# A batched product of 96 heads: where the pieces stored apart are multiplied and copied

## The chip, the cores and the metric

The kernel runs on one core of a Trainium2 chip. Its time is device microseconds of one execution. The median of three runs before the change is 300.72 us (300.61 to 300.89).

## The reference

```python
batch, n_heads, seq_t, seq_s, channels = 8, 12, 512, 512, 64
def reference(x, y):            # x: b h t c, y: b h s c, float32
    return np.einsum('bhtc,bhsc->bhts', x, y).astype(np.float32)
```

There are 96 heads. For each, the 512x64 matrix x is multiplied by the transpose of the 512x64 matrix y, which gives 512x512 numbers. 25 MB are read and 100 MB are written.

## The kernel before

The heads are worked off in six loads of 16 heads, for x and for y (`load`, line 157). ScalarE, VectorE and GpSimd turn them to bf16 in one large SBUF tensor, `keep` (`compress`). Each load gives two halves, so there are 12 halves `i` (0 to 11). For each half, `mix` copies x into `xb` in an order fit for the transposes, and `transposes` lets VectorE turn it into `xT` (line 206) and y into `yT` (line 215). `xT` and `yT` exist twice, for even and odd halves.

Each half holds four heads for each of two output rows: the output has 48 tiles `o`, four to a half. A tile is 128 partitions of 4096 numbers, 2 MB. It is made in two halves of four products each (128x128 by 128x512): the first in the PSUM buffer `pm0`, the second in `pm1` (`four`, line 234). Each PSUM buffer is four banks, and the two fill PSUM. ScalarE evicts each half into one of five SBUF slots (`result`, line 337), and SyncE stores the slot (`store`, line 328). A slot is free for another tile when its store has landed.

The order on each engine is written out by hand. `need` finds which semaphores an engine must wait for, and `emit` records who wrote and who reads each buffer. Only TensorE's program is a loop: `all_products` runs six turns of eight tiles each (two halves), and what must run once stands in it as a block under a condition on the turn; `emit(..., held=...)` collects the steps of that block in place of issuing them. Behind the last tile of each half, `prepare` issues the transposes of a later half and the `mix` copies of the one after it.

Tile 41 (`SPLIT`) is stored in parts. All its odd partitions (1 MB) and the first quarter of its even ones (256 KB) leave from the slot. The rest, 64 rows of 12 KB, is made once more in other partitions: `corner` gathers the columns of `xT` that belong to these rows into `picked` (three VectorE copies, line 275), multiplies them by `yT` in 30 products of 96 or 16 columns, four to a group (line 295, eight groups), copies each group into a part of `keep` that is free by then (`kept`, lines 139 and 141), and sends these rows in three transfers: 20 rows by SyncE, 12 and 32 by GpSimd (line 314). The three gathers and the products stand behind tile 41. The groups alternate between `pm0`, copied by VectorE, and `pm1`, copied by ScalarE. TensorE leaves the block when the last copies are done, and only then goes on with tile 42. SyncE issues its 20 rows ahead of the store of tile 42.

Of the kernel before, what the change touches and what calls it, by code (L numbers as in the profile page):

```python
# [9 lines left out]
def kernel(  # L10
# [22 lines left out]
    nc = tc.nc  # L33
    B, H, T, C = x.shape
    _, _, S, _ = y.shape
# [3 lines left out]
    R = T // Q  # L39
# [9 lines left out]
    LEFT = 6  # L49
    N = (K - LEFT) * S  # L50
    GROUP = 4
    FEW = ((0, 4, 5), (5, 8, 4), (16, 24, 4))
    fp32 = mybir.dt.float32
    bf16 = mybir.dt.bfloat16
    u32 = mybir.dt.uint32
# [52 lines left out]
    def emit(name, make, reads=(), writes=(), dma=None, lane=None, known_by=None, held=None):  # L108

        points = [writer[r] for r in (*reads, *writes) if r in writer]  # L110
        points += [v for w in writes for v in readers.get(w, ())]
        if name == "pool" and name in ticks:
            points.append((name, ticks[name]))
        need(name, points, known_by, held)
        p, step = (lane or name, 1) if dma is None else (f"dma{dma}", 16)
        if p not in sems:
            sems[p] = tc.alloc_semaphore(p)
        if held is not None:
            held.append(make)
        elif make is not None:  # L120
            make().then_inc(sems[p], step)
        at = (p, ticks.get(p, 0) + step)
        ticks[p] = at[1]
        snaps[at] = {**known[name], p: at[1]}
        if dma is None:
            for q in lanes.get(name, (name,)):
                snaps[at][q] = ticks.get(q, 0)
        for r in reads:
            readers.setdefault(r, []).append(at)
        for w in writes:  # L130
            writer[w], readers[w] = at, []

    made_slots, loaded, held = [], {}, []
    in_front = ["dve", "pool", "dve", "act"]

    def copy(name, dst, src, reads, writes):
        emit(
            name,
            lambda: nc.scalar.activation(dst, src, COPY)  # L139
            if name == "act"  # L140
            else engines[name].tensor_copy(dst, src),  # L141
            reads,
            writes,
        )
# [95 lines left out]
    def all_products():  # L240

        with nc.tensor.Fori(0, TURNS, 1) as t:
            for j in range(2 * V):
                if j % V == 0:
                    nc.tensor.wait_ge(sems["tr"], t * 2 + j // V + 1)
                for pm in range(2):
                    nc.tensor.wait_ge(sems["ev"], t * (4 * V) + 2 * j + pm + 1)
                    four(j, pm).then_inc(sems["pe"], 1)
                if j == SPLIT % (2 * V):
                    with nc.tensor.If(t == SPLIT // (2 * V)):  # L250
                        for step in held:
                            if callable(step):
                                step().then_inc(sems["pe"], 1)
                            else:
                                nc.tensor.wait_ge(sems[step[0]], step[1])

    def corner():

        half, h = divmod(SPLIT % (2 * V), V)
        xT = xTs[half].bitcast(bf16).rearrange("p (k h q u) -> p k h q u", k=K, h=V, u=2)  # L260
        yT = yTs[half].bitcast(bf16)
        most = max(many for _, _, many in FEW)
        kept = keep[:, :most * LEFT * S].bitcast(fp32)
        runs = kept.rearrange("p (j n) -> p j n", j=most)
        dst = ov[SPLIT // V, h][:, 0, N:]
        picked = keep[:, 3 * NG * R // 2 * D:].bitcast(bf16)[:, :most * LEFT * 96].rearrange(
            "p (j k m) -> p j k m", j=most, k=LEFT
        )
        under = [("yb", 1, b, ch) for b in range(NG - 3, NG - 1) for ch in range(2)]
        first = 0  # L270
        for lo, hi, many in FEW:
            rows = (hi - lo) * many
            emit(
                "dve",
                lambda: nc.vector.tensor_copy(  # L275
                    picked[:, :many, :, 4 * lo:4 * hi:4],
                    xT[:, K - LEFT:, h, first:first + rows, 0].rearrange("p k (e j) -> p j k e", j=many),
                ),
                [("xT", half)],
                [("picked", lo)] + (under if lo == 0 else []),  # L280
            )
            first += rows
        places = [[("xk", i)] for i in range(NG - 1)]
        for i in range(0, NG - 1, 2):
            places.append([("yb", 0, b, ch) for b in (i, i + 1) if b < NG - 1 for ch in range(2)])
        banks = [divmod(b, LEFT) for b in range(most * LEFT)]
        for g in range(0, len(banks), GROUP):
            part = banks[g:g + GROUP]
            pm = g // GROUP % 2
            m = 96 if part[0][0] < most - 1 else 16  # L290

            def make(part=part, pm=pm, m=m):

                for b, (j, k) in enumerate(part):
                    last = nc.tensor.matmul(  # L295
                        pms[pm][:m, b, :], picked[:, j, k, :m], yT[:, h * S:(h + 1) * S],
                        start=True, stop=True,
                    )
                return last

            emit("pe", make, [("picked", lo) for lo, _, _ in FEW] + [("yT", half)], [("pm", pm)], held=held)
            copy(
                "act" if pm else "dve", kept[:m, g * S:(g + len(part)) * S],
                pms[pm].rearrange("p j s -> p (j s)")[:m, :len(part) * S],
                [("pm", pm)], places[g // GROUP],
            )
        need("pe", [v for pm in range(2) for v in readers[("pm", pm)]], held=held)
        first = 0
        for lo, hi, many in FEW:
            rows = (hi - lo) * many  # L310
            name = "pool" if lo else "sp"
            emit(
                name,
                lambda: engines[name].dma_start(  # L314
                    dst[first:first + rows].rearrange("(e j) n -> e j n", j=many),
                    runs[4 * lo:4 * hi - 3:4, :many],
                ),
                reads=[w for place in places for w in place],
                dma="side" if lo else "corner",
            )  # L320
            first += rows
# [24 lines left out]
    def prepare(i):  # L346

        if i < NH:
            transposes(i)
        if i + 1 < NH:  # L350
            for part in range(4):
                mix(i + 1, "dve", part)

    with tc.tile_critical():  # L354
        sems["ev"] = tc.alloc_semaphore("ev")
        ticks["ev"] = 2
        nc.scalar.sem_inc(sems["ev"], 2)
        for g in range(SLOTS):
            load(g)
        emit(  # L360
            "pool",
            lambda: nc.gpsimd.dma_start(  # L362
                spare[0:17:4, :, :D // 2], xv[0, 0:5].rearrange("p (a b c) -> p a b c", a=2, c=D)[:, :, 0, :D // 2]
            ),
            writes=["spare"],
            dma="side",
        )
        for half, name in enumerate(("dve", "pool")):
            emit(
                name,  # L370
                lambda: engines[name].memset(xbs[half], 0.0),  # L371
                writes=[("xb", half, part) for part in range(4)],
            )
        front = []
        for n in range(2 * NG):
            if n == 11:
                result(3, slot())
            compress(n)
            mix(n // 4, "pool", n % 4)
            if n == 4:  # L380
                transposes(0)
            if n < 5:
                load(n + SLOTS)
            elif n in (6, 8):
                load(n // 2 + 7)
            elif n < 10:
                front.append(slot())
            if n > 7 and n < 11:
                result(n - 8, front[n - 8])
            if n == 9:  # L390
                transposes(1)
        prepare(2)
        for o in range(V, V * NH):
            result(o, slot())
            if o == SPLIT:
                corner()
            if o % V == V - 1:
                prepare(o // V + 2)
        all_products()
        need("pool", [("dmaside", ticks["dmaside"])])  # L400
        need("dve", [("dmacorner", ticks["dmacorner"])])
        for i, name in enumerate(("dve", "dve", "dve", "dve", "act")):
            need(name, [(f"dma{i}", ticks[f"dma{i}"])])
# [30 lines left out]
```

## Time and profile before

| | |
|---|---|
| median of three runs | 300.72 us |
| the profiled execution | 300.63 us |
| its span in the trace | 298.8 us |
| mean granted TensorE clock | 0.77 |
| moved by DMA | 125.87 MB, mean 421 GB/s |
| busy: TensorE, VectorE, ScalarE, GpSimd | 48%, 54%, 73%, 19% |
| ScalarE's evictions (line 337) | 96, 173.7 us, mean 1894 ns |
| VectorE's copies of pieces | 4, mean 2285 ns |
| ScalarE's copies of pieces | 4, mean 1657 ns |
| TensorE's products for pieces (line 295) | 30, 9.2 us busy |

A row of the profile names the engine, the line of the kernel, the operation, and what it writes and reads. PE is TensorE's matmul, PEld its weight load, DVE is VectorE, ACT ScalarE, POOL GpSimd, SP SyncE; a "q" behind the name is its sequencer. In brackets stands the idle time of the engine before the row, and what ended it. The slices cut the span in 40 equal parts of 7.47 us; digits are tenths busy, PEclk is the granted clock in tenths. Times are counted from the span's start.

### The profile page before, as it was taken

Reading aid. Unit: us, or ns where it says so; the run is one execution under the profiler, and the core shown is the slowest. Engines: PE = TensorE matmul, PEld = TensorE weight load, DVE = VectorE, ACT = ScalarE, POOL = GpSimd, SP = SyncE. Lnnn points to the kernel's source line nnn. Section 1 sums busy time; section 2 is a strip of 40 time slices with the busy share of each in tenths; the row PEclk is TensorE's granted clock in tenths of the full one; section 3 lists DMA queues with packets and bytes.
Section 4 is the critical chain, followed back from the end, with each engine's and each line's share of the span. In section 5 each row is a group of like instructions: output and inputs, shape, how many; then the busy total and the mean of one; then the engine's idle time right before and its main releaser. Section 6 shows DMA issues by size and latency. Waiting matters only on the chain.

```text
span 298.8 us, 1363 instructions
## 1 busy us (share of the span) xinstructions
PE 144.7 (48%) x408; PEld 39.3 (13%) x414; DVE 161.6 (54%) x80; ACT 217.9 (73%) x113; POOL 57.9 (19%) x26
## 2 busy tenths in 40 slices
PE   0000040547665663867475665676475667475400
PEld 0000010111111110211111111111111112121100
DVE  2167897999929594915809439076292535600000
ACT  1665676999999996786868686767777775589900
POOL 3399999991000000000000000000000000010000
PEclk9999995657789997565956767756857767979965
DMA  7999999999999999999999999999999999999997
GB/s 265 430 428 432 430 430 428 428 432 432 425 432 430 434 428 429 434 430 428 430 432 429 432 436 428 430 436 423 425 432 434 430 421 428 421 388 430 421 421 316
DMA packets 8875, 125.87 MB, mean 421 GB/s; under 512 B 1128, under 2 KB 1128, under 8 KB 1192
## 3 DMA queue, kind: packets, MB, share of 16 engines
q1 hardware_dynamic: 8680, 125.29, 98.6%
q0 software_dynamic: 192, 0.54, 0.5%
q8 instruction: 1, 0.02, 0.0%
q14 instruction: 2, 0.02, 0.0%
HBM read 25.17 MB, written 100.66 MB: 421 GB/s over the span
## 4 chain that ended last, share of the span: by engine, by line
DMA 54%; ACT 27%; issue 5%; PE 4%; DVE 3%; another core or an unknown queue 1%; SPq 0%; ACTq 0%
DMA out_dram<-slot 41%; ACT slot L337 25%; DMA slot<-in_y_dram 7%; DMA slot<-in_x_dram 6%; DVE keep L141 3%; ACT keep L139 2%; PE pm L295 2%; PE pm L234 2%; SPq L157 0%; ACTq L101 0%; SPq L429 0%; SPq L354 0%
## 5 line engine op out<-in xcount | busy, mean ns | idle before, releaser
L337 ACT ACTIVATE slot<-pm 128x2048 f32<-128x2048 f32 x96 | 173.7, 1894 | 38.2 <-DMA out_dram<-slot 35.0
L234 PE MATMUL pm<-yT,xT 128*128 128x512 bf16 x378 | 135.6, 502 | 132.0 <-ACT slot L337 92.4
L206 DVE STREAM_TRANSPOSE xT<-xb 128x2048 uint32<-128x2048 uint32 x12 | 46.8, 3897 | 69.4 <-PE pm L234 67.0
L234 PEld LDWEIGHTS pm<-yT,xT 128*128 128x128 bf16 x384 | 35.9, 114 | 230.7 <-ACT slot L337 152.0
L139 ACT ACTIVATE keep<-slot 128x4096 bf16<-128x4096 f32 (+1 forms) x12 | 36.5, 3044 | 21.5 <-DMA slot<-in_x_dram 16.3
L141 DVE COPY xb<-keep 32x2048 bf16<-32x2048 bf16 x36 | 47.0, 1305 | 1.0
L141 DVE CAST keep<-slot 64x2048 bf16<-64x2048 f32 x12 | 36.1, 3010 | 17.1 <-DMA slot<-in_y_dram 16.9
L314 POOL DMA_DIRECT2D out_dram<-keep x2 | 1.1, 558 | 192.6 <-DVE keep L141 192.6
L141 POOL COPY xb<-keep 32x2048 bf16<-32x2048 bf16 x12 | 36.2, 3017 | 9.2 <-ACT keep L139 8.4
L215 DVE STREAM_TRANSPOSE yT<-keep 128x1024 uint32<-128x1024 uint32 x12 | 23.1, 1928 | 0.0
L141 POOL CAST keep<-slot 64x2048 bf16<-64x2048 f32 x6 | 17.8, 2973 | 1.4 <-DMA slot<-in_y_dram 0.8
L141 DVE COPY keep<-pm 96x2048 f32<-96x2048 f32 (+1 forms) x4 | 9.1, 2285 | 10.5 <-PE pm L295 10.5
L295 PE MATMUL pm<-yT,keep 128*96 128x512 bf16 (+1 forms) x30 | 9.2, 446 | 4.9 <-DVE keep L141 2.8
L139 ACT ACTIVATE keep<-pm 96x2048 f32<-96x2048 f32 (+1 forms) x4 | 6.6, 1657 | 5.4 <-PE pm L295 5.4
L295 PEld LDWEIGHTS pm<-yT,keep 128*96 128x96 bf16 (+1 forms) x30 | 3.4, 130 | 11.0 <-DVE keep L141 4.5
L371 DVE MEMSET xb<- 128x2048 uint32 x1 | 1.8, 1765 | 1.4 <-SPq L354 1.4
L139 ACT ACT_TABLE_LOAD x1 | 1.3, 1283 | 1.0 <-SPq L354 1.0
L371 POOL MEMSET xb<- 128x2048 uint32 x1 | 1.8, 1823 | 0.0
L362 POOL DMA_DIRECT2D spare<-in_x_dram x1 | 0.7, 701 | 1.2 <-SPq L354 1.2
L275 DVE COPY keep<-xT 128x120 bf16<-128x120 bf16 (+2 forms) x3 | 0.7, 355 | 0.0
L418 POOL MEMSET const-float32-0.0<- 128x1 f32 x1 | 0.1, 98 | 0.2 <-issue 0.2
L418 POOL MEMSET const-float32-1.0<- 128x1 f32 x1 | 0.1, 98 | 0.0
(2 smaller groups left out, 0.2 us busy)
## 6 DMA issues: line engine op xcount, KB each, us to landing
out_dram<-slot SPq DMA_DIRECT2D x47, 2048.0 KB, 20.5
slot<-in_x_dram SPq DMA_DIRECT2D x6, 2048.0 KB, 17.7
slot<-in_y_dram SPq DMA_DIRECT2D x6, 2048.0 KB, 20.8
out_dram<-slot SPq DMA_DIRECT2D x1, 1024.0 KB, 16.9
out_dram<-keep POOLq DMA_DIRECT2D x1, 384.0 KB, 6.1
out_dram<-slot SPq DMA_DIRECT2D x1, 256.0 KB, 18.6
out_dram<-keep SPq DMA_DIRECT2D x1, 240.0 KB
out_dram<-keep POOLq DMA_DIRECT2D x1, 144.0 KB, 5.6
```

The lines of the kernel that those rows point to most:

```text
L139: lambda: nc.scalar.activation(dst, src, COPY)
L141: else engines[name].tensor_copy(dst, src),
L206: lambda: nc.vector.transpose(xTs[half].rearrange("p (k r e) -> p k e r", k=K, e=E), xbs[half].rearrange("p (k e c) -> p k e c", k=K, e=E),),
L215: lambda: nc.vector.transpose(yTs[half].rearrange("p (r j) -> p j r", r=D), ybs[half][b].rearrange("p (j c) -> p j c", c=D),),
L234: last = nc.tensor.matmul(pms[pm][:, b, :], xT[:, 4 * pm + b, h, :], yT[:, h * S:(h + 1) * S], start=True, stop=True,)
L275: lambda: nc.vector.tensor_copy(picked[:, :many, :, 4 * lo:4 * hi:4], xT[:, K - LEFT:, h, first:first + rows, 0].rearrange("p k (e j) -> p ...
L295: last = nc.tensor.matmul(pms[pm][:m, b, :], picked[:, j, k, :m], yT[:, h * S:(h + 1) * S], start=True, stop=True,)
L314: lambda: engines[name].dma_start(dst[first:first + rows].rearrange("(e j) n -> e j n", j=many), runs[4 * lo:4 * hi - 3:4, :many],),
L337: lambda: nc.scalar.activation(slots[s][:, k * S:(k + 4) * S], pms[pm].rearrange("p j s -> p (j s)"), COPY),
L362: lambda: nc.gpsimd.dma_start(spare[0:17:4, :, :D // 2], xv[0, 0:5].rearrange("p (a b c) -> p a b c", a=2, c=D)[:, :, 0, :D // 2]),
L371: lambda: engines[name].memset(xbs[half], 0.0),
L418: nc = _bacc.Bacc("TRN2", target_bir_lowering=False, num_devices=1)
```

## The change

The eight groups no longer stand behind tile 41. One group is made behind each of the tiles 37 to 44, in a block of its own in TensorE's loop, so that each of the eight places of the loop has a condition and a block. All groups use `pm0`, and all are copied by VectorE. The next tile's first half, which uses `pm0` too, is multiplied after that copy. The gathers (`pick`) move to behind tile 35, after `prepare`, in which the half with tile 41 is transposed; on VectorE they now precede the transposes that are issued behind tile 39. The three transfers (`send`) are issued behind the store of tile 44; the SyncE one was ahead of the store of tile 42 and is now ahead of the store of tile 45. The transposes behind tile 39 stand on VectorE between the copies of the groups of tiles 39 and 40. ScalarE copies none of the pieces any more. The products, their number, the rows of the transfers and the bytes are the same.

```diff
+    BEGIN = SPLIT - 4
+    GROUPS = -(-max(many for _, _, many in FEW) * LEFT // GROUP)
...
-                if j == SPLIT % (2 * V):
-                    with nc.tensor.If(t == SPLIT // (2 * V)):
-                        for step in held:
-                            if callable(step):
-                                step().then_inc(sems["pe"], 1)
-                            else:
-                                nc.tensor.wait_ge(sems[step[0]], step[1])
+                for o in held:
+                    if o % (2 * V) == j:
+                        with nc.tensor.If(t == o // (2 * V)):
+                            for step in held[o]:
+                                if callable(step):
+                                    step().then_inc(sems["pe"], 1)
+                                else:
+                                    nc.tensor.wait_ge(sems[step[0]], step[1])
...
-        for g in range(0, len(banks), GROUP):
-            part = banks[g:g + GROUP]
-            pm = g // GROUP % 2
...
-            copy(
-                "act" if pm else "dve", kept[:m, g * S:(g + len(part)) * S],
-                pms[pm].rearrange("p j s -> p (j s)")[:m, :len(part) * S],
-                [("pm", pm)], places[g // GROUP],
-            )
-        need("pe", [v for pm in range(2) for v in readers[("pm", pm)]], held=held)
+    def piece(o):
+        g = o - BEGIN
...
+            for b, (j, k) in enumerate(part):
+                last = nc.tensor.matmul(
+                    pms[0][:m, b, :], picked[:, j, k, :m], yT[:, h * S:(h + 1) * S],
+                    start=True, stop=True,
+                )
...
+        held[o] = []
+        emit(
+            "pe", make, [("picked", lo) for lo, _, _ in FEW] + [("yT", half)], [("pm", 0)], held=held[o]
+        )
+        copy(
+            "dve", kept[:m, g * GROUP * S:(g * GROUP + len(part)) * S],
+            pms[0].rearrange("p j s -> p (j s)")[:m, :len(part) * S],
+            [("pm", 0)], places[g],
+        )
+        need("pe", readers[("pm", 0)], held=held[o])
...
         for o in range(V, V * NH):
             result(o, slot())
-            if o == SPLIT:
-                corner()
+            if BEGIN <= o < BEGIN + GROUPS:
+                piece(o)
+            if o == BEGIN + GROUPS - 1:
+                send()
             if o % V == V - 1:
                 prepare(o // V + 2)
+            if o == BEGIN - 2:
+                pick()
```

## Prediction

> **What bounds the kernel now.** I read the page first, then the waits, then the order of time around tile 41, then cut that stretch into fine windows. The page's slices show a kernel that waits for its transfers:
>
> ```profile
> PEclk9999995657789997565956767756857767979965
> DMA  7999999999999999999999999999999999999997
> GB/s 265 430 428 432 430 430 428 428 432 432 425 432 430 434 428 429 434 430 428 430 432 429 432 436 428 430 436 423 425 432 434 430 421 428 421 388 430 421 421 316
> ```
>
> The DMA engines are full from the second slice to the last but one. The only dent is slice 36 (261.5 to 268.9 us, 388 GB/s). So only work that opens or closes a hole in the transfers moves the time. The waits agree: ScalarE's most frequent wait is for a store to leave its slot.
>
> ```profile
> ACT slot L337 <- DMA out_dram<-slot: 35.0, 28, 2.5
> DVE keep L141 <- PE pm L295: 10.5, 4, 6.2
> ```
>
> Next the order of time (start, us, engine, line, operation) around the pieces:
>
> ```profile
> 224.80 3.65 ACT L337 ACTIVATE slot<-pm 128x2048 f32<-128x2048 f32 x2 [1.31 <-DMA out_dram<-slot]
> ...
> 239.54 3.65 ACT L337 ACTIVATE slot<-pm 128x2048 f32<-128x2048 f32 x2 [1.25 <-DMA out_dram<-slot]
> ...
> 244.49 3.65 ACT L337 ACTIVATE slot<-pm 128x2048 f32<-128x2048 f32 x2 [1.30 <-DMA out_dram<-slot]
> ...
> 246.51 1.03 PE L295 MATMUL pm<-yT,keep 128*96 128x512 bf16 x4 [1.38 <-ACT slot L337]
> 247.59 2.29 DVE L141 COPY keep<-pm 96x2048 f32<-96x2048 f32 x1 [6.16 <-PE pm L295]
> ...
> 258.76 2.28 DVE L141 COPY keep<-pm 16x2048 f32<-16x2048 f32 x1 [1.12 <-PE pm L295]
> ...
> 261.40 0.84 PE L234 MATMUL pm<-yT,xT 128*128 128x512 bf16 x3 [2.25 <-DVE keep L141]
> ...
> 262.71 21.35 ACT L337 ACTIVATE slot<-pm 128x2048 f32<-128x2048 f32 x12 [2.51 <-remote]
> ...
> 266.38 18.24 SPq L328 DMA_DIRECT2D out_dram<-slot  x6
> ```
>
> The rows at 224.80, 239.54 and 244.49 are the evictions of tiles 37, 40 and 41: one tile every 4.92 us, the rate of the stores. The pieces then hold tile 42 until 262.71, some 13 us behind that rate. A store lands 20.5 us after its issue (the page's DMA issues), so about three tiles of transfers are queued and nearly cover this. What they don't cover is this hole (last columns: granted clock, DMA share, GB/s):
>
> ```profile
> 266.30:266.70 0.40, 0.29 (x2) 0.17 (x3) 0.00 (x0) 0.40 (x2) 0.00 (x0) 1.00 0.45 174
> 266.70:267.10 0.40, 0.40 (x4) 0.14 (x2) 0.00 (x0) 0.40 (x1) 0.00 (x0) 1.00 0.25 92
> 267.10:267.50 0.40, 0.35 (x2) 0.00 (x0) 0.00 (x0) 0.40 (x1) 0.00 (x0) 1.00 0.09 31
> 267.50:267.90 0.40, 0.00 (x0) 0.00 (x0) 0.00 (x0) 0.40 (x1) 0.00 (x0) 1.00 1.54 655
> ```
>
> That is (0.55 + 0.75 + 0.91) x 0.4 = 0.88 us, a mean over 16 engines. It is the most the change can win: 0.3%. In the packet records the last engine ends its pieces at 267.64, when the store of tile 42 already begins (about 267.7), so the engine that ends last has next to no hole, and the likely prize is 0 to 0.25 us.
>
> **What the change costs, part by part.** It makes a piece behind each of tiles 37 to 44, always in pm0, always copied by VectorE. Before, pm0 and pm1 took turns. Now the first half of tile o+1 can't be multiplied until the piece of tile o has left pm0. That puts a chain into each tile:
>
> - ScalarE starts on pm0, to the piece's first product: 2.02 us (244.49 to 246.51; an ordinary group follows after 1.94, 239.54 to 241.48, so entering the block shows at most 0.1).
> - The piece's four products: 1.08 us to the copy's start at full clock (246.51 to 247.59), 1.80 at half clock (248.19 to 249.99, where ScalarE takes the second group).
> - VectorE's copy: 2.30 us with its hand-off (2285 ns in the page).
> - Copy's end to the next tile's first product, out of the block: 261.04 to 261.40, 0.36 us.
> - The tile's four products to ScalarE's start: 1.08 us at full clock, 1.93 at half (66.77 to 68.70 in the chain that ended last).
>
> The sum is 6.84 us a tile at full clock and 8.41 at half, against 4.92 for the stores. ScalarE, PE's sequencer and SP queue behind it: tile o+1's eviction waits on PE, its store waits on that eviction.
>
> Which clock? Rows of 3.41 us, cut where the granted clock may change (PE busy, count, granted clock):
>
> ```profile
> 238.17:241.58 3.41, 1.99 (x5) 0.50 1.05 447
> 241.58:245.00 3.42, 3.42 (x8) 0.50 0.98 417
> 245.00:248.41 3.41, 1.38 (x6) 1.00 1.02 432
> 248.41:251.82 3.41, 3.41 (x8) 0.50 1.03 437
> 251.82:255.24 3.42, 2.10 (x10) 1.00 0.98 417
> ```
>
> A stretch with 8 or more products is followed by full clock, one with 4 to 6 by half. The ordinary tiles make 8 products in 4.92 us, 5.5 a stretch, and the clock there is 0.66 on average: full one third of the time. The new chain makes 12 products in 6.84 to 8.41 us, 6.0 to 4.9 a stretch: the same kind of work, somewhat thinner at half clock. I take a quarter full: 8.41 - 0.25 x 1.57 = 8.0 us. The ends 6.84 and 8.41 stay for the range.
>
> Tile 37 starts at 224.80 as before, and seven such steps put tile 44's eviction at 224.80 + 56.0 = 280.8. The two transposes for tiles 44 to 47 (5.6 us, 235.20 to 240.83) now stand on VectorE between the copies of tiles 39 and 40. At 8.0 us there are 5.7 us between copies, so they fit; at full clock, with 4.5, they add 1.1 once.
>
> From there the transfers set the end. Eviction start to store issue is 3.65 us, and issue to first packets 1.3 (266.38 to about 267.7): 285.75. Tile 44's store takes 4.93 (six stores from 267.7 to the last packet at 297.3), ending at 290.7. The pieces' 768 KB come only now: 1.83 us at 430 GB/s if spread evenly, 2.33 if the 20-row transfer's five rows per engine set the pace (12 KB packets took 0.467 us; it signals completion from four engines only). I take 2.3, since the holes in front level the engines. Tiles 45 to 47 need 14.8 more: 307.8, against 297.3 before, so +10.5. Their evictions are on time: tile 45's store is ready 5.5 to 6.5 us behind tile 44's, and the transfers take 7.2 over that stretch.
>
> The rest costs nothing, and this covers it. The three gathers (0.73 us) move to behind the mixes, which end at 225.84, so they end at 226.57, before tile 37's piece could start (226.82); uncovered, 0.7 once. ScalarE loses four copies (6.6 us) that no store waits for any more. SP's piece transfer moves past the stores of tiles 42, 43 and 44 to ahead of tile 45; its copy ends about when tile 44's store issues, so it holds nobody. GpSimd's two have nothing behind them. All turns of PE's loop now test a condition after each tile; PE idles over a microsecond per ordinary tile, and a delay there would first eat the queued stores.
>
> The profiled execution took 300.63 us for its span of 298.8; 300.63 + 10.5 = 311.1, and the median shown is 0.09 higher: 311.2 us.
>
> **The Trainium skill against this sum.** In this trace the clock halves although PE idles for no more than about 2.2 us between groups of ordinary tiles. The Trainium skill, "TensorE: Matmul & The Clock Gate", Part 1, has it that the clock drops only after about 3.4 us of idleness. By that rule the new chain, whose longest idle time is the copy and the exit, 2.7 us, stays at full clock; the rows here speak against it, but it is the first rival.
>
> **The rivals.** (1) Full clock throughout: 7 x 6.84 + 1.1 puts tile 44 at 273.8, the end at 300.8, +3.5: 304.2 us. For it: the clock was full for 10 us inside the block of pieces. Against: products were denser there (30 in 15 us). (2) Not slower: the queued stores cover the delays. Without its pieces behind it tile 41's store ends at about 264.7, tiles 42 and 43 at 274.5, so tile 44 may start as late as 274.5 - 4.95 = 269.6, a step of at most 6.4 us. The best sum is 6.84, so this needs overlap that I don't see (0.44 us less a tile in all). Then the hole closes and the time is 299.8 to 300.6; it is the rival on the other side. (3) Entering and leaving the block eight times costs more. At 245.1 PE was through with tile 41 and began the piece at 246.51; up to 1.4 us of this may be the jump and not the wait for ScalarE. At half clock PE is through only 0.5 us before ScalarE is, so up to 0.9 more a tile, 6 us in all: 317 us. The page's instruction queues moved 3 packets in the whole span, and none stands near the block, so I hold it unlikely. The Trainium skill ("Runtime: NRT & Kernel Launch", Instruction fetch mechanics) warns that a taken branch can force a fetch of code; no row here shows one.
>
> **How the numbers follow.** Mostly half clock: 0.62, time 311.2, its own span 307 to 314.1 (all half: tile 44 at 283.7, +13.4). Full clock: 0.20. Costly branches: 0.12. Queue covers all: 0.06. The range leaves out the last two and takes in the others: 303.8 to 314.6. A measurement here tells about 0.2% (0.6 us) from no change. Faster by more needs the whole mean hole: 0.02. Within: 0.04. Slower: 0.94.
>
> **What would show it.** In the profile after: evictions from tile 37 on at a pitch of 7 to 8.4 us, not 4.92; ScalarE waiting there for PE, PE for VectorE's copy; holes in the transfers from about tile 41 on (slices 35 to 38 well under 400 GB/s); granted clock mostly 0.5 between 225 and 280; the last store issued near 295. A pitch under 6.4, or slices that stay at 420 to 430, would prove the whole sum wrong; a pitch near 6.8 with the clock at 1.0 would prove rival 1.

## The result, and the profile after

The changed kernel takes 311.15 us (median of 6 runs, 310.36 to 311.94) against 300.67 before (300.55 to 300.97). The ratio is 1.0347, with a 95% interval of 1.0328 to 1.0367: slower by 3.5%. The profiled execution took 311.66 us with a span of 309.9; both are 11.0 us more than in the profiled execution before.

The page's slices of the changed kernel, now 7.75 us each:

```profile
PEclk9999999879899985577677659557756776775875
DMA  7999999999999999999999999999999998366997
GB/s 273 436 429 423 434 429 423 431 434 425 434 429 431 427 434 433 429 431 429 434 428 431 431 431 427 427 434 431 419 436 425 429 431 362 163 271 271 429 410 311
```

Up to slice 33 the transfers run as before. Slices 34 to 37 (255.7 to 286.7 us) are the loss: 163 GB/s in the worst. The waits (us in total, times, longest) name the two links of a chain: ScalarE waits for TensorE, and TensorE for VectorE's copy.

```profile
ACT slot L349 <- PE pm L236: 34.0, 9, 5.7
...
PE pm L236 <- DVE keep L143: 21.0, 8, 3.2
```

In the kernel before, these two waits are hardly there:

```profile
PE pm L234 <- DVE keep L141: 2.2, 1, 2.2
...
ACT slot L337 <- PE pm L234: 0.6, 3, 0.2
```

In order of time (start, us, engine, line, operation, what ended the idle time), from tile 37 to tile 39:

```profile
224.90 3.65 ACT L349 ACTIVATE slot<-pm 128x2048 f32<-128x2048 f32 x2 [1.30 <-DMA out_dram<-slot]
226.83 0.79 DVE L279 COPY keep<-xT 128x120 bf16<-128x120 bf16 x3
...
227.67 1.94 PE L299 MATMUL pm<-yT,keep 128*96 128x512 bf16 x4 [2.26 <-DVE keep L279]
229.65 2.29 DVE L143 COPY keep<-pm 96x2048 f32<-96x2048 f32 x1 [2.03 <-PE pm L299]
232.30 3.59 PE L236 MATMUL pm<-yT,xT 128*128 128x512 bf16 x8 [2.69 <-DVE keep L143]
234.22 3.65 ACT L349 ACTIVATE slot<-pm 128x2048 f32<-128x2048 f32 x2 [5.68 <-PE pm L236]
...
236.15 1.71 PE L299 MATMUL pm<-yT,keep 128*96 128x512 bf16 x4 [0.26 <-ACT slot L349]
237.90 2.29 DVE L143 COPY keep<-pm 96x2048 f32<-96x2048 f32 x1 [5.96 <-PE pm L299]
240.55 3.28 PE L236 MATMUL pm<-yT,xT 128*128 128x512 bf16 x8 [2.69 <-DVE keep L143]
242.16 3.65 ACT L349 ACTIVATE slot<-pm 128x2048 f32<-128x2048 f32 x2 [4.29 <-PE pm L236]
```

Tile 38's step can be read off: eviction starts at 234.22, the piece's products at 236.15 (1.93 later), the copy at 237.90 (1.75), its end is 240.19, the next tile's products start at 240.55 (0.36), the next eviction at 242.16 (1.61). The evictions of tiles 37 to 45 start at 224.90, 234.22, 242.16, 250.32, 257.93, 265.86, 273.65, 281.30 and 287.83. At the other end the engines of the transfers stand still while the store of a tile is awaited (last columns: granted clock, DMA share, GB/s):

```profile
265.00:270.00 5.00, 3.78 (x10) 1.09 (x8) 0.92 (x1) 3.65 (x2) 0.00 (x0) 0.68 0.14 56
...
280.00:286.00 6.00, 3.88 (x9) 0.96 (x9) 1.21 (x1) 3.65 (x2) 0.19 (x1) 0.50 0.51 218
```

### The profile page after: what moved, and what is told of

The parts are those of the page before. It is cut to its first block, busy times and chain, and to the rows that moved or that the text cites. A ratio compares the mean times of both kernels' runs of the same rounds, so it can differ in the third digit from the quotient of the medians.

```text
span 309.9 us, 1408 instructions
## 1 busy us (share of the span) xinstructions
PE 153.5 (50%) x408; PEld 41.8 (13%) x414; DVE 169.7 (55%) x84; ACT 211.7 (68%) x109; POOL 57.9 (19%) x26
## 4 chain that ended last, share of the span: by engine, by line
DMA 45%; ACT 24%; DVE 11%; PE 11%; issue 6%; SPq 0%; ACTq 0%; DVEq 0%
DMA out_dram<-slot 32%; ACT slot L349 21%; DVE keep L143 7%; PE pm L236 7%; DMA slot<-in_y_dram 7%; DMA slot<-in_x_dram 6%; PE pm L299 4%; ACT keep L141 2%; DVE xb L143 2%; DVE xT L208 1%; DVE yT L217 1%; SPq L159 0%; DVE keep L279 0%; ACTq L103 0%; SPq L445 0%
## 5 line engine op out<-in xcount | busy, mean ns | idle before, releaser
L236 PE MATMUL pm<-yT,xT 128*128 128x512 bf16 x378 | 142.5, 524 | 138.1 <-ACT slot L349 79.0
L236 PEld LDWEIGHTS pm<-yT,xT 128*128 128x128 bf16 x384 | 38.1, 118 | 240.2 <-ACT slot L349 134.8
L143 DVE COPY keep<-pm 96x2048 f32<-96x2048 f32 (+2 forms) x8 | 17.2, 2151 | 35.1 <-PE pm L299 35.1
L299 PE MATMUL pm<-yT,keep 128*96 128x512 bf16 (+1 forms) x30 | 11.0, 499 | 4.5 <-DVE keep L279 2.3
```

Of the source, the lines that this page charges most:

```text
L236: last = nc.tensor.matmul(pms[pm][:, b, :], xT[:, 4 * pm + b, h, :], yT[:, h * S:(h + 1) * S], start=True, stop=True,)
L299: last = nc.tensor.matmul(pms[0][:m, b, :], picked[:, j, k, :m], yT[:, h * S:(h + 1) * S], start=True, stop=True,)
```

## The experiments

My theory: each tile from 37 on waits through pm0 for VectorE's copy of the piece; this makes a step of 6.8 to 8.4 us where the stores need 4.92, and the half clock is a good part of the step. The rivals: the eight blocks and branches or the later place of the transfers cost; the clock plays no part. A side question: what is the hole before worth, and can another place of the pieces win it?

**Without the copy.**

```diff
     def piece(o):
...
-        copy("dve", kept[...], pms[0]..., [("pm", 0)], places[g])
-        need("pe", readers[("pm", 0)], held=held[o])
+        known["pe"]["pe"] = ticks["pe"]
```

The added line tells `need` that TensorE need not wait for its own products.

> The changed kernel without VectorE's eight copies out of pm0, and so without TensorE's wait for them; the eight blocks of products and the three transfers stay where the change puts them (the pieces' rows then hold old data). If the chain through that copy is the cause, a tile's step is 2.0 + 1.1 to 1.8 + about 0.3 + 1.1 to 1.9, so 4.5 to 6.0 us, under the 6.4 that the queued stores allow: 300.3 to 301.0 us. Rival, the eight blocks themselves or the later place of the transfers cost: 304 us or more. Rival, the products: still well over 301.

Measured: 300.18 us against 300.57 before on the same chip, ratio 0.9989 (0.9979 to 0.9999). Its slices 33 to 39 show no hole:

```profile
GB/s 272 433 428 433 428 428 428 426 419 442 428 422 426 441 428 423 433 439 426 430 433 434 422 433 437 428 426 433 437 424 424 428 428 428 424 428 426 426 428 290
```

Blocks, branches, products and the late transfers are all still there, and the whole loss is gone: tile 44 starts at 259.80. The rival that they cost falls, and so does my third rival of the prediction.

**Half the copy.**

```diff
-            "dve", kept[:m, g * GROUP * S:(g * GROUP + len(part)) * S],
-            pms[0]...[:m, :len(part) * S],
+            "dve", kept[:m, g * GROUP * S:(g * GROUP + len(part) // 2) * S],
+            pms[0]...[:m, :len(part) // 2 * S],
```

> The changed kernel with only the first half of each group copied (VectorE's copy 1.2 us in place of 2.29; the other half of the pieces' rows holds old data). A dose: if the copy stands on the chain of each tile, the steps shrink from 7.85 to about 6.8 us, tile 44 starts some 7.5 us earlier than in the changed kernel, and the time is 303.7 us (302.5 to 305). If only having a wait there counts and not its length: 309 to 311.

Measured: 302.29 us (301.14 to 303.78), ratio 1.0054 (1.0034 to 1.0073), a little under the expected range. The copies took 1.22 us; the steps were 7.37 once and then 6.53 to 7.01, tile 44 started at 272.11. The length of the copy counts, not only that there is one. The step shrank by more than the copy (7.85 to 6.6 after the first): the granted clock between tile 38 and tile 44 was 0.75 (232 to 274 us), against 0.71 in the changed kernel (232 to 281 us), and I had reckoned with the same clock.

**The clock, first try: the second group twice.**

```diff
                     nc.tensor.wait_ge(sems["ev"], t * (4 * V) + 2 * j + pm + 1)
+                    if pm:
+                        four(j, pm)
                     four(j, pm).then_inc(sems["pe"], 1)
```

> The changed kernel with every tile's second group of four products made twice (same result), in all tiles. These repeats lie beside ScalarE's eviction of the first half and add no length to the chain at full clock. If the clock follows the count of products per 3.41 us, 16 products a step keep it at 1.0, the steps fall to about 6.9 us, and the time to 304.5 us (303.5 to 306), with a narrower spread from run to run. If the clock is not part of the loss: 311. If it stays at half in spite of them, the piece comes later: 315 to 321.

Measured: 312.32 us (310.17 to 313.23), ratio 1.039 (1.034 to 1.044): a miss. The same edit on the kernel before is the control:

> The control for the repeated products: the kernel before with every tile's second group made twice. The clock is then near 1.0 in all stretches between 60 and 285 us, and since the transfers set the time it stays at 300.4 to 301.0 us. If the clock bounded the kernel before, it would be faster by more than 0.6 us.

Measured: 301.81 us (301.07 to 302.1), ratio 1.0048 (1.0031 to 1.0064): a miss by 0.8 us, so the repeats are not free even there. Of the first the trace tells why:

```profile
279.44 1.88 ACT L351 ACTIVATE slot<-pm 128x2048 f32<-128x2048 f32 x1 [4.01 <-PE pm L236]
282.86 1.88 ACT L351 ACTIVATE slot<-pm 128x2048 f32<-128x2048 f32 x1 [1.54 <-PE pm L236]
```

These are the two evictions of tile 44. Four of the steps took 7.0 to 7.3 us, but in the others the clock fell to half all the same, and then the repeats delay the second half: it starts 3.42 us after the first in place of 1.78. The edit lengthens what it was to leave alone, so it tells nothing clean about the clock.

**The clock, second try: products in a gap.** While VectorE copies, pm1 is empty and TensorE has nothing to do.

```diff
+        def filler():
...
+        emit("pe", filler, [("yT", half)], [("pm", 1)], held=held[o])   # four products into pm1, used by nobody
+        known["pe"]["pe"] = ticks["pe"]
         need("pe", readers[("pm", 0)], held=held[o])
```

> The changed kernel with four more products in each of the eight blocks, into pm1 once ScalarE has emptied it, while VectorE copies the piece out of pm0 (their result is overwritten by the next tile and used by nobody). They end before the copy does even at half clock, so they add nothing to the chain, and make 16 products a step. If the half clock is the rest of the loss, the clock stays near 1.0, the steps fall to about 6.9 us, tile 44 starts near 276 and the time is 305.8 us (304.5 to 307), with less spread from run to run. If the clock plays no part: 311. If the filler holds TensorE up: over 312.

Measured: 305.64 us (304.45 to 306.5), ratio 1.0163 (1.0136 to 1.019). The two kernels over the same stretch, first with the filler, then the changed one (PE busy, products, granted clock, DMA share, GB/s):

```profile
224.00:283.00 59.00, 36.42 (x132) 0.92 0.92 388
```

```profile
224.00:283.00 59.00, 35.13 (x87) 0.67 0.86 366
```

45 more products stand in the records of the same 59 us, and the time is 5.5 us shorter: the clock rises from 0.67 to 0.92. The last steps are 6.84, 6.75, 6.75 and 6.81 us, which is the full-clock sum of the prediction:

```profile
254.96 3.65 ACT L361 ACTIVATE slot<-pm 128x2048 f32<-128x2048 f32 x2 [3.19 <-PE pm L236]
261.71 3.65 ACT L361 ACTIVATE slot<-pm 128x2048 f32<-128x2048 f32 x2 [3.11 <-PE pm L236]
268.46 3.65 ACT L361 ACTIVATE slot<-pm 128x2048 f32<-128x2048 f32 x2 [3.11 <-PE pm L236]
```

What moves the clock? In these traces the granted clock changes only after 3.41 us or a multiple of it. Four such stretches of the changed kernel (PE busy, products, granted clock, DMA share, GB/s):

```profile
257.97:261.38 3.41, 3.15 (x8) 0.50 1.00 428
261.38:264.80 3.42, 0.73 (x4) 1.00 0.75 316
264.80:268.21 3.41, 3.15 (x8) 0.50 0.22 87
268.21:271.62 3.41, 0.83 (x4) 1.00 0.36 154
```

Between 224 and 299 us of this trace all 7 stretches with 8 or more products are followed by full clock, and all 13 with 6 or fewer by half. (With 7 products it goes either way in these traces.) TensorE idles there for some 2.7 us at a time between two groups, once 3.2, and its clock was half for two thirds of the time. The filler also shortens these idle times, so by itself it doesn't tell idle time from work. The kernel with the second group twice does: it idles for 3.16 us from 244.33 to 247.49 and keeps full clock:

```profile
242.39:245.80 3.41, 1.70 (x7) 1.00 0.93 394
245.80:249.22 3.42, 1.73 (x8) 1.00 1.06 450
249.22:252.63 3.41, 2.09 (x9) 1.00 0.95 404
```

The Trainium skill ("TensorE: Matmul & The Clock Gate", Part 1) has in its table that the clock falls after an idle window of about 3.4 us; these runs don't agree with that as the only way, as it falls here around idle times of 2.7 us. What they fit is the amount of work per 3.41 us.

**The transfers of the pieces.**

```diff
-            if o == BEGIN + GROUPS - 1:
-                send()
...
-        need("dve", [("dmacorner", ticks["dmacorner"])])
```

> The changed kernel without the three transfers of the pieces (their 64 rows are not sent). If they come only behind the holes, and so lie on the path of the slowest transfer engines with their whole 2.3 to 2.45 us: 308.7 us (308.0 to 309.4). If they fill holes or even out the engines as before: 310.5 to 311.2.

Measured: 310.48 us (310.0 to 311.26), ratio 1.0322 (1.0303 to 1.0342), against 1.0347 with them. A miss: only 0.7 us less, where I expected 2.4. Without the pieces the engines come to a stop behind tile 44's store, since tile 45's is not there yet:

```profile
291.00:292.50 1.50, 0.81 (x4) 0.31 (x4) 0.00 (x0) 1.50 (x2) 0.00 (x0) 1.00 0.01 0
```

In the changed kernel the same 1.5 us moved 369 GB/s, nearly all of it pieces. They fill a hole that the next wait would open: tile 45's eviction starts 6.53 us behind tile 44's in both kernels. In the packet records of this run tile 44's store ends at 291.39 and tile 45's first packet starts at 292.85, a hole of 1.46 us. Only what of the pieces' 2.3 us goes beyond it lies on the path, some 0.9 us. The intervals of the two ratios overlap, so the 0.7 us of the medians is not resolved from nothing; it is clear of 2.4.

**The gathers earlier.**

```diff
     def prepare(i):
         if i < NH:
             transposes(i)
+        if i == SPLIT // V:
+            pick()
         if i + 1 < NH:
...
-            if o == BEGIN - 2:
-                pick()
```

> The changed kernel with the three gathers on VectorE ahead of the four mixes behind tile 35 in place of behind them. In the changed kernel the first piece started 0.8 us later than ScalarE allowed, since the gathers were late. If that is on the path, the time falls by about 0.8 to 310.4 us; the spread of the runs (1.6 us) may hide part of it. If later steps take it back: 311.2.

Measured: 311.05 us (309.61 to 311.42), ratio 1.034 (1.0319 to 1.0361). The first piece now starts 2.03 us behind tile 37's eviction, as summed, and tile 38's eviction 7.77 us behind tile 37's in place of 9.32. But the medians of these two kernels differ by 0.1 us and their ranges overlap: whether it helps the time is not decided by these runs.

**What the hole is worth.** The kernel before without the pieces' products and copies:

```diff
...
-            emit("pe", make, ..., [("pm", pm)], held=held)
-            copy("act" if pm else "dve", kept[...], pms[pm]..., [("pm", pm)], places[g // GROUP])
-        need("pe", [v for pm in range(2) for v in readers[("pm", pm)]], held=held)
```

> The kernel before without the products and the copies of the pieces (the gathers and the three transfers stay behind tile 41, the pieces' rows hold old data). The most that any other place for the pieces can win. If the hole is worth what the last engine loses: 300.4 to 300.7 us. If its mean: 299.8.

Measured: 300.10 us (300.0 to 300.2) against 300.55, ratio 0.9983 (0.9975 to 0.9992). So the most to be won is about 0.45 us: more than the 0 to 0.25 that I read from the last engine, half of the mean hole.

**Two blocks of four.**

```diff
+    HERE = {BEGIN: range(0, 4), SPLIT: range(4, 8)}
...
+        for g in HERE[o]:
+            pm = g % 2
...
+                "act" if pm else "dve", kept[...], pms[pm]..., [("pm", pm)], places[g],
...
-            if BEGIN <= o < BEGIN + GROUPS:
+            if o in HERE:
                 piece(o)
-            if o == BEGIN + GROUPS - 1:
+            if o == SPLIT:
                 send()
```

> The eight groups in two blocks of four, behind tile 37 and behind tile 41, alternating pm0 with VectorE and pm1 with ScalarE as in the kernel before; gathers behind tile 35, transfers behind tile 41. Each block holds ScalarE's next tile some 6.5 us, less than the queue of stores covers, and three tiles at 3.65 us in place of 4.92 win part of it back in between, so the hole near 267 us should close. If the hole is worth only what the last transfer engine loses in it: 300.4 to 300.7 us, no or hardly any gain. If it is worth its mean: 299.8.

Measured: 301.15 us (300.35 to 301.38), ratio 1.0016 (1.0008 to 1.0025): a miss, slower. Yet in the profile the hole is closed, slices 33 to 39 move 415 to 435 GB/s, and the span is 298.5 us, below the 298.8 before. What grew is the time around the span (the time less the span): 2.05 to 3.0 us in these runs, against 1.73 to 1.86 in 23 runs of the kernel before. The queues of the page say where to look:

```profile
q1 hardware_dynamic: 8680, 125.29, 98.7%
q0 software_dynamic: 192, 0.54, 0.5%
q14 instruction: 2, 0.02, 0.0%
```

The kernel before has one instruction packet of 16 KB on q8 as well, at 115 us. Here this packet comes too, but 1.7 us behind the span's end. (An 8 KB packet of q14 comes 1.0 to 1.9 us behind the span's end in every run; only the one of q8 is new there.) The kernel without the pieces' products, whose TensorE program is shorter, has no packet on q8 at all. I took it for a piece of TensorE's program, which the edit had changed, and tried to move it by lengthening the program:

```diff
+        for _ in range(24):                       # 64 in the second run
+            nc.tensor.wait_ge(sems["ev"], 1)
         with nc.tensor.Fori(0, TURNS, 1) as t:
```

> The kernel with two blocks of four groups, with 24 waits that are already met ahead of TensorE's loop, which only lengthens its program. In the two blocks' run the span was 298.5 us, shorter than before, but 2.05 to 3.0 us lay around it in place of 1.8, and a 16 KB instruction packet came only behind the span's last instruction. If the packet's place goes with the length of TensorE's program, it moves into the loop and the time falls to 300.2 us; if 24 are too few, it stays at 301.15.

> The same with 64 such waits. If the packet's place goes with the length of TensorE's program, it comes during the loop as in the kernel before and the changed one, and the time is 300.2 us, below the kernel before. If the time around the span has another reason: 301.15.

Measured: 300.11 us with 24 waits (ratio 0.9984, 0.9975 to 0.9994) and 300.16 with 64 (0.9988, 0.9979 to 0.9997), against 300.63 before. With 24 the packet is back in the span, at 81 us, and with 64 as well:

```profile
q8 instruction: 1, 0.02, 0.0%
q14 instruction: 2, 0.02, 0.0%
```

The time around the span is 1.8 us again. So the packet's place and that time went together in three versions. How the packet costs the time is not shown: in the profiled execution of the two blocks its record ends 2.7 us behind the span's end, but only 2.4 us lay around the span. Nothing is left out of these two versions, and they beat the kernel before by 0.5 us, as much as the kernel without any products for pieces.

## Why the prediction was right

The forecast was 311.2 us for the chain at mostly half clock, in a range of 303.8 to 314.6; measured were 311.15. The mechanism is right; that the two numbers agree to 0.05 us is luck, as the six runs spread over 1.6 us and the profiled one, from which the steps below are read, took 311.66.

- **The chain.** Right, step by step. Into the block 2.02 was summed, 1.93 measured; the copy 2.30, measured 2.29; out of the block 0.36, measured 0.36 to 0.45, but 0.83 behind tile 39, where TensorE's loop turns: 0.47 that I had not priced. Taking the copy away takes the loss away; halving it removes most of it.
- **The clock.** I took a quarter of the time at full clock, for a step of 8.0. Measured: seven steps in 56.4 us, 8.06 on average. It fits partly by chance. The gathers ended at 227.62, not 226.57, as the transposes ahead of them had waited for a half-clock group; the cover of 0.25 us was gone and the first piece 0.75 late. I had named this price and counted it at nothing. Without it and the 0.47 the mean step is 7.88, which is one third at full clock, the share of the ordinary tiles. Against 1.08 us each, the measured groups of tiles 38 to 44 and pieces 37 to 43 lost 5.2 and 2.6 us to the clock: by this sum 7.8 of the 11. The filler kernel confirms the kind and won 5.5 back, at a clock of 0.92.
- **From tile 44 to the end.** The sum said: time after minus time before is tile 44's start minus 270.3 (the end before, 297.3, less 27.0). The profiled runs: 281.30 gives 11.0, measured 11.0; half the copy, 272.11 gives 1.8, measured 1.8; filler, 275.27 gives 5.0, measured 5.0; gathers first, 279.61 gives 9.3, measured 9.4. The 2.3 us for the pieces in it are right as a length (2.3 from the end of tile 44's store), but of this only some 0.7 to 0.9 would vanish with the pieces, since tile 45's store was the next to be late. I had checked that it was on time behind the pieces, and not what stood behind it. One sign was off: the last store was issued at 298.58, not near 295. Tile 45 comes 6.53 us behind tile 44, and the transfers were still busy with the stores ahead of it, so this cost nothing.
- **Not slower, the rival on the other side.** It fell, at the limit that I had worked out: a step of at most 6.4 us. Half the copy, at 6.53 to 7.01, is just above and loses 1.7 us; no copy, at 4.9 on average, is below and loses nothing.
- **The prize.** Mis-sized: 0 to 0.25 us summed, 0.45 to 0.5 measured. Why the last engine gains more than its own hole was not tried.

## What to carry to other kernels

Work that is spread over many steps is hidden only if each step has room for it: compare the new chain per step with the pace of the bound, and the sum of what it exceeds with the queue in front of the bound. A buffer that took turns and now does not turns two overlapping copies into a chain. When a span shrinks and the time does not, look at what lies around the span.

## What the runs showed of the hardware

TensorE's clock follows the work in stretches of 3.41 us: in the changed kernel, between 224 and 299 us, 8 or more products in a stretch were followed by full clock and 6 or fewer by half (20 of 20 stretches). 12 products in about 7.9 us left it at 0.67, 16 in 6.8 us at 0.92, so that useless products made a kernel 5.5 us faster. One 16 KB instruction packet fell behind the last instruction of the span in one version, and 2.05 to 3.0 us lay around the span there in place of 1.8; 24 idle waits moved it into the loop, where no cost of it shows (301.15 against 300.11 us). The Trainium skill ("Runtime: NRT & Kernel Launch", Instruction fetch mechanics) calls the crossing of a 16 KB boundary mostly hidden; the version with the packet at the end, with its 2.05 to 3.0 us, fits that badly. That the packet belongs to TensorE's program is inferred from this, not seen.
